# A decoder layer on one Trainium2 core: seven block products in the fourth gate-and-up tile of the FFN too, and the splits it needs in one row

## The chip, the cores and the metric

The kernel runs on 1 core of one Trainium2 chip, as one launch. The metric is the device time of a launch in microseconds (us). Unless said otherwise, times inside a launch are counted from the first instruction of one profiled execution. The engines are called by the profile's names: PE (TensorE matmul) with PEld (its weight load), DVE (VectorE), ACT (ScalarE), POOL (GpSimd) and SP (SyncE, which here issues DMAs).

## What is computed

One layer of a decoder for a prompt of 512 tokens and a sample group of 8 sequences with one token each, 520 tokens in all, width 1024. All tensors are float32. Cut to what matters here:

```python
D_FF = 2816
x = x + g1 * mixed                                    # after the RG-LRU and attention branches, @ w_o
h2 = rms_norm(x, norm2_g) * (1.0 + sc2) + sh2
gu, up = jnp.split(h2 @ w_ffn_in, 2, axis=-1)
x = x + g2 * ((jax.nn.silu(gu) * up) @ w_ffn_out)
y = rms_norm(x, normf_g)
```

## The kernel before, in words

**Layout.** Activations are held transposed, 128 features on the partitions and the 520 tokens along the free dimension, cut into two halves of 260 tokens (`HALVES`). Every matmul is 128x128 weights against 128x260 tokens. Float32 products are made of three fp32r matmuls: weights and activations are each split into a rounded part "hi" (a cast on ACT) and the rest "lo" (a subtraction on DVE), and hi\*hi, lo\*hi and hi\*lo are summed.

**The FFN.** The 2816 gate columns and 2816 up columns are worked in 22 tiles `jt` of 128 gate and 128 up columns. The main loop's head treats tiles 0 and 1 together (names `fi0` to `fi3`, first all four products of the first token half, then all four of the second; meanwhile `rstd_half` and `h2_half(1)`, L1434 to L1458, make the second half of the FFN input `h2`). Tiles 2 and 3 are plain tiles (`ffn_tile`): a gate product `fig` and an up product `fiu`, each of 8 k-tiles x 3 matmuls x 2 halves = 48 matmuls. From tile `GROUP` = 4 on, `fast_tile` (L1588) treats the tile as a 2x2 by 2x2 block product (gate and up columns; the two halves of k; the two halves of the tokens) and needs seven block products of 4 k-tiles x 3 matmuls = 12 matmuls each, in place of eight. The seven stand in the order of `BLOCKS`: A11, S2, S3, S1, A12, A22, S4. Their results meet in four PSUM banks X, Y, W and Z, with two ACT copies and four DVE additions (L1601, L1616, L1622).

**What the seven products need.** On the weight side, four block sums S1 to S4 of each tile, made on POOL by `split_block` (L264 to L267, each 128x512, results in `ws` tiles), and one split of each block into hi and lo by `split_four` (ACT L273, DVE L274, names `wb`). On the activation side, block sums of `h2` in `u` and `w`, made once on POOL by `h2_blocks` (L1580 to L1583, sixteen instructions of 128x260), and their splits `tu` and `tw`, made once by `split_blocks` (ACT L341, DVE L342, eight pairs of 128x520). A11, A12 and S4's activation operands are blocks of `h2` itself; S2 and S3 use `tw`, S1 and A22 use `tu`. S2, the second product of a tile, uses all four `tw`.

**When things are issued.** `begin` asks for the loads and splits of the units that lie ahead: loads 22 and splits 11 in a unit of time near a microsecond. `split_upto(first + m - 1)` at the end of the head already asks for the splits of the next three units. `defer(k, fn)` puts a function behind the k-th product from here. `split_blocks` stands under `issue_after(state["silu"].ins)`: its ACT instructions come behind the last silu before it. Each weight chunk of 1024 rows by 256 columns is loaded by SP into one of two `wraw` buffers; the next chunk but one waits until a buffer's readers are done. Split weights have three `whi` and three `wlo` buffers, `ws` and other large tiles seven (`pg`), most other tiles come from a heap of 60 slots.

**The order on an engine** isn't that of the program text alone: when the program is built, a scheduler that walks through estimated time gives each engine the earliest instruction in the text whose inputs it takes to be ready. On the chip each engine then keeps that order strictly, and waits where an input is late.

From tile 4 on, products `fo` of the second FFN matrix stand behind blocks S2 and A12 (`JOIN`): those in tiles 4 to 7 use the finished tiles 0 to 3, and so on.

Of the kernel before, what the change touches and what calls it, by code (L numbers as in the profile page):

```python
# [65 lines left out]
def kernel(ctx, tc, xT, par, gates, b_f, cst, cse, own, cache_k, cache_v, cache_lf, pt,  # L66
# [13 lines left out]
    def slot(name, cols=NT, dt=F32, parts=128):  # L80
        return heap.tile([parts, cols], dt, name=name, tag="slot")

    def bank(name, parts=128, cols=512):
        return psp.tile([parts, cols], F32, name=name, tag="bank")
# [32 lines left out]
    def cols(src, c0, n=256, k0=0, nk=KT):  # L117
        return [(src, k0, nk, c0, n)]
# [22 lines left out]
    for i in range(0, KT, 2):  # L141
        chunks.append(cols(w_o, 128 * i))
    GROUP = 4
    PLAIN = 2
    LAST = 16
    JOIN = {}
    for jt in range(GROUP, LAST):
        JOIN[jt] = {"S2": (jt // GROUP - 1, 2 * (jt % GROUP)), "A12": (jt // GROUP - 1, 2 * (jt % GROUP) + 1)}
    for i, (jt, name) in enumerate(((16, "S2"), (16, "A12"), (17, "A12"), (18, "A12"), (19, "A12"), (20, "A12"),
                                    (21, "S2"), (21, "A12"))):  # L150
        JOIN.setdefault(jt, {})[name] = (LAST // GROUP - 1, i)
    BLOCKS = ("A11", "S2", "S3", "S1", "A12", "A22", "S4")
    units = []

    def whole(c):
        for o in range(0, sum(p[4] for p in chunks[c]), 128):
            units.append((c, o, chunks[c][0][2]))
# [4 lines left out]
    for jt in range(FF // 128):  # L162
        c = len(chunks)
        chunks.append(cols(w_fi, 128 * jt, 128) + cols(w_fi, FF + 128 * jt, 128))
        if jt < GROUP:
            whole(c)
            continue
        for name in BLOCKS:
            units.append((c, name, 4))
            if name in JOIN[jt]:  # L170
                g, i = JOIN[jt][name]
                if i % 2 == 0:
                    joined.add(len(chunks))
                    chunks.append(cols(w_fo, 128 * i, 256, 128 * GROUP * g, GROUP))
                units.append((max(joined), 128 * (i % 2), GROUP))
    for i in range(0, KT, 2):
# [108 lines left out]
    def defer(k, fn):  # L285
        later.setdefault(state["n"] + k, []).append(fn)

    def begin(last=None):
        n = state["n"]
        state["n"] += 1  # L290
        last = len(units) - 1 if last is None else last
        if n < 42:
            tick(KEYS[n], n in VALUES)
        load_chunks(units[reach(n, last, state["load"])][0])
        split_upto(reach(n, last, state["lead"]))
        flush()
        return n
# [13 lines left out]
    def run_later(n):  # L311
        for fn in later.pop(n, []):
            fn()
# [7 lines left out]
    def product(name, a, evac, mid=None):  # L321
        n = begin()
        for j in range(2):
            b = bank(f"{name}_{j}")
            half_product(n, j, a, b)
            evac(j, b[:, :HALF])
            if j == 0 and mid is not None:
                mid()
        run_later(n)
# [7 lines left out]
    def split(name, raw, scale=None):  # L337
        hi = slot(name + "h", dt=F32R)
        lo = slot(name + "l", dt=F32R)
        if scale is None:  # L340
            act.copy(hi, raw)  # L341
            dve.tensor_tensor(lo, raw, hi.bitcast(F32), ALU.subtract)  # L342
        else:
            act.activation(hi, raw, AF.Copy, scale=scale)
            dve.scalar_tensor_tensor(lo, raw, scale, hi.bitcast(F32), ALU.mult, ALU.subtract)
        return hi, lo
# [1070 lines left out]
    def residual(f, ps, gate, j):  # L1417
        if j == 0:
            dve.scalar_tensor_tensor(x[f][:, :HALF], ps[:, :HALF], mod[:, gate, f, 0:1], x[f][:, :HALF],
                                     ALU.mult, ALU.add)  # L1420
            return
        n = NP - HALF
        t = small("rs", 128, NS)
        dve.tensor_tensor(t, ps[:, n:HALF], mod[:, gate, f, 1:9], ALU.mult)
        dve.scalar_tensor_tensor(x[f][:, HALF:NP], ps[:, :n], mod[:, gate, f, 0:1], x[f][:, HALF:NP],
                                 ALU.mult, ALU.add)
        dve.tensor_tensor(x[f][:, NP:], x[f][:, NP:], t, ALU.add)
# [32 lines left out]
    def split_part(dst, src, part=slice(None)):  # L1460
        hi, lo = dst
        act.copy(hi[:, part], src)
        dve.tensor_tensor(lo[:, part], src, hi[:, part].bitcast(F32), ALU.subtract)
# [34 lines left out]
    def swish(b, t, j):  # L1498
        t0, t1 = HALVES[j]
        state["silu"] = act.activation(t[:, t0:t1], b[:, :HALF], AF.Silu)  # L1500

    def times_up(b, t, j):
        t0, t1 = HALVES[j]
        dve.tensor_tensor(t[:, t0:t1], b[:, :HALF], t[:, t0:t1], ALU.mult)
# [53 lines left out]
    def pair_out():  # L1558
        return slot("ach", dt=F32R), slot("acl", dt=F32R)

    def ffn_tile(jt):
        t, out = slot("sw"), pair_out()
        product(f"fig{jt}", h2, lambda j, b: swish(b, t, j))

        def up(j, b):
            t0, t1 = HALVES[j]
            times_up(b, t, j)
            split_part(out, t[:, t0:t1], slice(t0, t1))

        product(f"fiu{jt}", h2, up)  # L1570
        return out
# [14 lines left out]
    def split_blocks(k0):  # L1586
        with tc.issue_after(state["silu"].ins):
            for k in range(k0, k0 + 2):  # L1588
                u, w = traw[k]
                tb.append((split("tu", u), split("tw", w)))  # L1590

    def h2_block(name, k):
        pair, part = {"A11": (h2[k], L_), "A12": (h2[k + 4], L_), "S4": (h2[k + 4], R_), "S1": (tb[k][0], L_),
                      "S2": (tb[k][1], L_), "S3": (tb[k][1], R_), "A22": (tb[k][0], R_)}[name]
        return [t[:, part] for t in pair]

    def fast_tile(jt, ac):
        sw, cp, u2, out = slot("sw"), slot("cp"), slot("u2", HALF), pair_out()
        X, Y, W, Z = (bank(f"fi{jt}{n}")[:, :HALF] for n in "xywz")
        into = {"A11": X, "S2": Y, "S3": W, "S1": Z, "A12": X, "A22": W, "S4": Z}  # L1600
        add = lambda o_, a_, b_: dve.tensor_tensor(o_, b_, a_, ALU.add)  # L1601

        def close(b, part):
            dve.tensor_tensor(b, b, sw[:, part], ALU.mult)
            split_part(out, b, part)

        for m_, name in enumerate(BLOCKS):
            n = begin()
            hi, lo = splits[n]
            for k in range(4):  # L1610
                ah, al = h2_block(name, k)
                for m, (wt, at) in enumerate(((hi, ah), (lo, ah), (hi, al))):
                    state["mm"] = pe.matmul(into[name], lhsT=wt[k], rhs=at, start=m_ < 4 and k == 0 and m == 0,
                                            stop=k == 3 and m == 2, skip_group_check=m_ > 3)
            if name == "A11":
                act.copy(cp[:, L_], X)  # L1616
            elif name == "S2":
                add(u2, cp[:, L_], Y)
            elif name == "S3":
                add(W, u2, W)  # L1620
            elif name == "S1":
                act.copy(cp[:, R_], Z)  # L1622
                add(Z, u2, Z)
                add(Y, cp[:, R_], W)
            elif name == "A12":
                act.activation(sw[:, L_], X, AF.Silu)
            elif name == "A22":
                close(W, L_)
            elif name == "S4":
                act.activation(sw[:, R_], Z, AF.Silu)  # L1630
                close(Y, R_)
            run_later(n)
            if name in JOIN[jt]:
                g, i = JOIN[jt][name]
                product(f"fo{g}_{i}", ac[GROUP * g:GROUP * g + GROUP], lambda j, b_, i=i: residual(i, b_, 5, j))
        return out

    ac, ts, ready = [], [slot("sw") for _ in range(PLAIN)], []
    u = state["n"]
    for j in range(2):  # L1640
        for m in range(2 * PLAIN):
            if j == 0:
# [10 lines left out]
            if j == 0 and m == 0:  # L1653
                h2_half(1)
            first = u + 2 * PLAIN
            if j == 0:
# [3 lines left out]
    for t in ts:  # L1660
        out = pair_out()
        split_part(out, t)
        ac.append(out)
    for jt in range(PLAIN, FF // 128):
        if jt == PLAIN:
            for k in range(4):
                h2_blocks(k)
            defer(0, lambda: split_blocks(0))
            defer(1, lambda: split_blocks(2))
        ac.append(fast_tile(jt, ac) if jt >= GROUP else ffn_tile(jt))  # L1670
    last_product(ac[LAST:])


# [60 lines left out]
```

## Time and profile before

| | us |
|---|---|
| median of 3 runs | 1031.36 |
| the three runs | 1032.33, 1027.59, 1031.36 |
| the profiled execution's own time | 1029.59 |
| its span, first to last instruction | 1027.9 |

The profile is one execution. Its page gives the busy time of each engine, a picture of the span in 40 slices, and the chain of waits that ended last; further views answer for a stretch of time, an engine or a tile. Rows of a timeline give start, duration, engine, line and operation, the output tile and its inputs, and in brackets how long the engine was idle before and what ended that. PE's rows overlap, since matmuls are pipelined: the time that a group of matmuls takes is read from the chain, which counts from one start to the next.

### The profile page before, as it was taken

What the parts mean: (1) busy time and instruction counts of PE and PEld (TensorE: products, weight loads), DVE (VectorE), ACT (ScalarE), POOL (GpSimd) and SP (SyncE); (2) the same over time, 40 slices, a digit from 0 to 9 for tenths busy, and PEclk for the clock granted to TensorE, in tenths of its full rate; (3) what the DMA queues carried; (4) which work ended last, traced back from release to release, by engine and by line L of the source; (5) the groups of instructions that cost most, each with busy time, mean ns of one, the idle gap of its engine ahead of it and who ended that gap; (6) DMA issues with size and microseconds to landing.
All of it is one profiled execution on the core that took longest, in us unless ns stands there. A gap on an engine that the chain in (4) does not pass through costs nothing.

```text
span 1027.9 us, 21296 instructions
## 1 busy us (share of the span) xinstructions
PE 992.3 (97%) x7994; PEld 918.8 (89%) x7994; DVE 796.8 (78%) x1423; ACT 551.0 (54%) x1132; POOL 328.6 (32%) x424
## 2 busy tenths in 40 slices
PE   4999999999999999999999999999999999999996
PEld 1788989999898988878888989999999999999996
DVE  5446999998989987886756544878888888888864
ACT  4433665857682267776875233565444444445453
POOL 0214511111133235654430001484432433434212
PEclk9899999999999999999999999999999999999998
DMA  9987987878888999988665784324243342333212
GB/s 323 307 280 285 306 290 217 261 233 276 261 254 310 323 314 306 310 259 274 219 235 185 252 302 126 83 62 115 71 124 99 87 124 72 93 104 103 62 63 84
DMA packets 165419, 206.99 MB, mean 201 GB/s; under 512 B 9906, under 2 KB 126146, under 8 KB 165250
## 3 DMA queue, kind: packets, MB, share of 16 engines
q1 hardware_dynamic: 148594, 152.52, 47.9%
q0 software_dynamic: 13040, 46.67, 13.7%
q10 hardware_dynamic: 3680, 6.42, 1.7%
q8 instruction: 63, 1.03, 0.4%
q14 instruction: 42, 0.34, 0.1%
HBM read 192.49 MB, written 13.09 MB: 200 GB/s over the span
## 4 chain that ended last, share of the span: by engine, by line
PE 70%; DVE 14%; DMA 6%; ACT 5%; issue 3%; SPq 0%; POOL 0%; POOLq 0%; DVEq 0%; ACTq 0%
PE fo L308 12%; PE pb L308 4%; PE gb L308 4%; PE ga L308 3%; PE k L308 3%; PE wo L308 3%; PE v L308 3%; DVE wlo L251 2%; DMA wraw<-in_w_in_dram 2%; PE gr L308 2%; PE xr L308 2%; DVE pg L733 2%; PE qp L530 2%; PE pv L818 2%; PE po L1261 2%
## 5 line engine op out<-in xcount | busy, mean ns | idle before, releaser
L249 ACT CAST whi<-wraw 128x1024 fp32r<-128x1024 f32 (+1 forms) x79 | 82.0, 1039 | 121.2 <-PE pb L308 35.1
L251 DVE TENSOR_TENSOR wlo<-wraw,whi 128x1024 fp32r<-128x1024 f32 (+1 forms) x79 | 101.3, 1284 | 32.6 <-ACT whi L249 30.5
L273 ACT CAST wb<-ws 128x512 fp32r<-128x512 f32 x72 | 44.8, 622 | 91.1 <-PE fo L308 63.6
L308 PE MATMUL fo<-ach,wb 128*128 128x260 f32 x512 | 93.3, 282 | 0.0
L685 POOL DMA_DIRECT2D pg<-in_cache_k_dram x74 | 39.4, 533 | 142.7 <-DVE S L734 70.3
L308 PEld LDWEIGHTS fo<-ach,wb 128*128 128x128 f32 x512 | 78.8, 188 | 0.0
L274 DVE TENSOR_TENSOR wb<-wraw,wb 128x512 fp32r<-128x512 f32 x86 | 74.2, 863 | 5.0 <-ACT wb L273 4.4
L274 DVE TENSOR_TENSOR wb<-ws,wb 128x512 fp32r<-128x512 f32 x72 | 65.8, 913 | 14.0 <-ACT wb L273 12.2
L264 POOL TENSOR_TENSOR ws<-wraw 128x512 f32<-128x512 f32 x18 | 26.6, 1480 | 153.8 <-DMA wraw<-in_w_fi_dram 124.8
L308 PE MATMUL fo<-acl,wb 128*128 128x260 f32 x256 | 72.3, 282 | 0.0
L273 ACT CAST wb<-wraw 128x512 fp32r<-128x512 f32 x86 | 53.6, 623 | 32.7 <-ACT cp L1622 5.8
L733 DVE TENSOR_TENSOR pg<-pg,qb 128x1024 f32<-128x1024 f32 x48 | 58.0, 1227 | 2.5 <-DMA pg<-in_cache_k_dram 2.4
L734 DVE TENSOR_REDUCE S<-pg 128x16 f32<-128x1024 f32 x48 | 57.0, 1207 | 0.1
L1218 POOL TENSOR_SCALAR p<-p,mu 128x128 f32<-128x128 f32 (+3 forms) x28 | 36.4, 1310 | 49.2 <-DVE mu L1214 31.3
L308 PEld LDWEIGHTS fo<-acl,wb 128*128 128x128 f32 x256 | 48.2, 188 | 0.0
L1212 ACT ACTIVATE p<-p,mu 128x128 f32<-128x128 f32 (+3 forms) x64 | 35.3, 553 | 15.9 <-DVE mu L1211 15.6
L308 PE MATMUL v<-hh,whi 128*128 128x260 f32 x128 | 37.3, 291 | 1.1 <-DVE pl L1232 1.1
L308 PE MATMUL pb<-oh,whi 128*128 128x260 f32 x128 | 36.7, 287 | 1.0 <-ACT oh L1319 1.0
L308 PE MATMUL k<-hh,whi 128*128 128x260 f32 x128 | 37.3, 291 | 0.0
L308 PE MATMUL gb<-hh,whi 128*128 128x260 f32 x128 | 37.0, 289 | 0.0
L308 PE MATMUL ga<-hh,wlo 128*128 128x260 f32 x128 | 36.3, 284 | 0.7 <-DVE wlo L251 0.7
L308 PE MATMUL pa<-gl,whi 128*128 128x260 f32 x128 | 36.1, 282 | 0.7 <-DVE gl L342 0.7
(1099 smaller groups left out, 3965.8 us busy)
## 6 DMA issues: line engine op xcount, KB each, us to landing
araw<-in_ada_w_dram SPq DMA_DIRECT2D x48, 512.0 KB, 7.0
wraw<-in_w_fi_dram SPq DMA_DIRECT2D x44, 512.0 KB, 4.7
pg<-in_cache_k_dram POOLq DMA_DIRECT2D x42, 512.0 KB, 6.0
pg<-in_cache_v_dram SPq DMA_DIRECT2D x42, 512.0 KB, 5.1
wraw<-in_w_in_dram SPq DMA_DIRECT2D x34, 512.0 KB, 7.8
wraw<-in_w_in_dram SPq DMA_DIRECT2D x11, 1024.0 KB, 10.0
pg<-in_cache_v_dram POOLq DMA_DIRECT2D x22, 512.0 KB, 6.4
pg<-in_cache_k_dram POOLq DMA_DIRECT2D x32, 256.0 KB, 5.7
```

Of the source, the lines that this page charges most:

```text
L249: state["act"] = act.copy(hi[:, :k1 - k0], src)
L251: state["last"] = dve.tensor_tensor(lo[:, :k1 - k0], src, hi[:, :k1 - k0].bitcast(F32), ALU.subtract)
L264: pool.tensor_tensor(s1, a21, a22, ALU.add)
L273: state["act"] = act.copy(t[:, :4], src)
L274: state["last"] = dve.tensor_tensor(t[:, 4:], src, t[:, :4].bitcast(F32), ALU.subtract)
L308: state["mm"] = pe.matmul(out[:, :t1 - t0], lhsT=wt[k], rhs=at, start=k == 0 and m == 0, stop=k == nk - 1 and m == 2)
L530: state["mm"] = pe.matmul(b[:, :HALF], lhsT=wt, rhs=at[:, t0:t1], start=k == 0 and m == 0, stop=k == 3 and m == 2)
L685: done.append(eng.dma_start(pg, cache[bass.ds(r, 1), :, c0:c1].rearrange("a p c -> (a p) c")))
L733: dve.tensor_tensor(pg, pg, q, ALU.mult)
L734: last = dve.tensor_reduce(S[r // 2][:, c:c + H], pg.rearrange("p (h d) -> p h d", d=DH), AX.X, ALU.add)
L1212: act.activation(p[:, :n + 128], p[:, :n + 128], AF.Exp, bias=mu[:, 0:1], scale=-1.0, accum_out=mu[:, 1:2])
L1218: (pool.tensor_scalar(p, p, mu[:, 2:3], None, ALU.mult) if a and i + 1 < KT else act.activation(p, p, AF.Copy, scale=mu[:, 2:3]))
```

## The change

- `FIRST = 3` takes the place of `GROUP` where it is decided which tiles are fast. Tile 3 becomes a fast tile. `GROUP` = 4 stays for the groups of `fo` products.
- The units of tile 3 are seven blocks in place of two plain units, with no `fo` product among them (`JOIN` has no entry for 3).
- Both calls of `split_blocks` stand behind the gate product of tile 2; before, the first call stood there and the second behind its up product.

```diff
     GROUP = 4
+    FIRST = 3
     PLAIN = 2
...
-        if jt < GROUP:
+        if jt < FIRST:
             whole(c)
             continue
...
-            if name in JOIN[jt]:
+            if name in JOIN.get(jt, ()):
...
             run_later(n)
-            if name in JOIN[jt]:
+            if name in JOIN.get(jt, ()):
...
-            defer(0, lambda: split_blocks(0))
-            defer(1, lambda: split_blocks(2))
-        ac.append(fast_tile(jt, ac) if jt >= GROUP else ffn_tile(jt))
+            defer(0, lambda: (split_blocks(0), split_blocks(2)))
+        ac.append(fast_tile(jt, ac) if jt >= FIRST else ffn_tile(jt))
```

## The prediction

> **What bounds the kernel now.** I read the busy table first, then the chain of waits over the stretch where the edit lies (655 to 720 us), then the timelines of POOL, DVE and SP there. The page's busy table:
>
> ```profile
> span 1027.9 us, 21296 instructions
> PE 992.3 (97%) x7994; PEld 918.8 (89%) x7994; DVE 796.8 (78%) x1423; ACT 551.0 (54%) x1132; POOL 328.6 (32%) x424
> ```
>
> PE is the bound over the whole, but the share says nothing about one stage. The chain says which wait ends last (columns: start, duration, what):
>
> ```profile
> 667.30 1.70 DVE r L409
> ...
> 669.52 0.33 POOL h2r L1450
> 669.92 0.28 POOL h2r L1451
> ...
> 677.51 8.44 PE fi L308 x68
> 685.95 5.74 PE fig L308 x48
> 691.68 5.74 PE fiu L308 x48
> 697.42 5.74 PE fig L308 x48
> 703.16 5.74 PE fiu L308 x48
> 708.90 1.43 PE fi4x L1613 x12
> ```
>
> Two things are to be seen. From 677.5 on the chain is PE without a gap: tile 2 (685.95), tile 3 (697.42), tile 4 (708.90, its first block product of seven). So a matmul less there is time less, as long as nothing is late. Before 677.5 the chain is not PE's: it runs through DVE, ACT **and two small POOL instructions**, the making of the second half of `h2`. PE waits for it little by little, and the whole list of PE's waits from 658 us to the end has only two rows beside it (engine, line, what it waited for: us in total, times, longest):
>
> ```profile
> PE r L407 <- DVE ss L400: 1.4, 1, 1.4
> PE fi L308 <- DVE h2l L1458: 1.1, 3, 0.4
> PE r L1536 <- ACT sq L1524: 0.2, 1, 0.2
> ```
>
> **The change part by part.**
>
> *Term 1, the matmuls.* Tile 3 goes from 2 x 48 = 96 matmuls to 7 x 12 = 84. Its chain rows give 5.74/48 = 0.120 us from one matmul to the next, and a block of 12 takes 1.43 to 1.44. So tile 3 takes 10.04 in place of 11.48: **-1.44 us**, 0.14% of the kernel. That is all the change can win; nothing else on the chain becomes shorter.
>
> *Term 2, four more block sums on POOL.* Tile 3 now needs S1 to S4 of its weights. They are asked for at the end of the head (the third of the three units that are split in advance there is now A11 of tile 3, whose call makes all four sums), that is in the text behind `h2_half(1)` and in front of `h2_blocks`. A tile's sums look like this, with what stands on POOL around them:
>
> ```profile
> 669.52 0.32 POOL L1450 TENSOR_TENSOR h2r<-h2r,n2amp 128x8 f32<-128x8 f32 x1 [9.64 <-DVE h2r L1446]
> ...
> 675.50 0.79 POOL L1582 TENSOR_TENSOR w<-h2r 128x260 f32<-128x260 f32 x1
> 676.24 0.92 POOL L1581 TENSOR_TENSOR w<-h2r,u 128x260 f32<-128x260 f32 x1
> ...
> 691.09 1.29 POOL L264 TENSOR_TENSOR ws<-wraw 128x512 f32<-128x512 f32 x1 [0.54 <-DMA wraw<-in_w_fi_dram]
> ...
> 695.43 2.15 POOL L267 TENSOR_TENSOR ws<-wraw,ws 128x512 f32<-128x512 f32 x1
> ```
>
> POOL idles 9.64 us before the first small instruction, and it doesn't keep the text's order: L1582 runs before L1581, which stands ahead of it, because L1581 needs the `u` that L1580 makes. So the scheduler will put the sums into that idle time if it takes tile 3's weights to be there. Are they? SP issues that chunk here, and the table by stretch shows the DMA share (next to last column) fall:
>
> ```profile
> 660.46 0.99 SPq L213 DMA_DIRECT2D wraw<-in_w_fi_dram  x2
> 663.00:665.00 2.00, 1.78 (x13) 1.75 (x14) 0.07 (x1) 1.97 (x3) 0.00 (x0) 1.00 1.18 317
> 665.00:667.00 2.00, 2.00 (x19) 2.00 (x18) 0.13 (x1) 1.09 (x2) 0.00 (x0) 1.00 0.22 50
> ```
>
> 0.22/1.18 of 2 us is 0.4, so the chunk is in at 665.4. Four sums at the undisturbed 1.29 take 5.2 and end at 670.6; at the 6.5 that the four took whose first and last are quoted (691.09 to 697.58) they end at 671.9. The small POOL instruction that is on the chain stands at 669.52. So the second half of `h2` is late by 670.6 - 669.5 = **1.1**, at most 2.4, and by nothing if the scheduler puts the sums behind. From 667.3 to 669.0 DVE works on the reciprocal, with one input, and has little else, so I take the undisturbed price, 1.1. That lateness goes to PE in full, since PE waits for that half already.
>
> *Term 3, the splits must be earlier.* Today `tw` is first used by tile 4's S2 at 708.90 + 1.43 = 710.33; now by tile 3's S2 at 697.42 + 1.44 = 698.86, and its fourth `tw` at the last three of the twelve matmuls, 698.86 + 11 x 0.12 = 700.2 for its lo part. The row of eight splits starts behind the silu of `fig2`:
>
> ```profile
> 691.72 0.39 ACT L1500 ACTIVATE sw<-fig 128x260 f32<-128x260 f32 x1 [2.35 <-PE fig L308]
> 692.66 1.54 DVE L342 TENSOR_TENSOR tul<-u,tuh 128x520 fp32r<-128x520 f32 x1 [2.71 <-ACT tuh L341]
> 694.12 2.32 DVE L251 TENSOR_TENSOR wlo<-wraw,whi 128x1024 fp32r<-128x1024 f32 x1
> 696.36 1.78 DVE L342 TENSOR_TENSOR twl<-w,twh 128x520 fp32r<-128x520 f32 x1
> 698.07 0.41 DVE L1504 TENSOR_TENSOR sw<-fiu,sw 128x260 f32<-128x260 f32 x1
> 698.41 0.68 DVE L342 TENSOR_TENSOR tul<-u,tuh 128x520 fp32r<-128x520 f32 x1
> 699.01 0.69 DVE L342 TENSOR_TENSOR twl<-w,twh 128x520 fp32r<-128x520 f32 x1
> ```
>
> ACT follows at 0.53 a cast and is no limit. A split on DVE takes 0.60 from start to start when POOL rests (698.41 to 699.01), but 1.5 to 1.8 beside POOL's sums of tile 4. Undisturbed, the three long DVE instructions from 692.66 to 698.07 are 0.6 + 1.2 (two 512s) + 0.6 = 2.4 us of work; they took 5.4, a rate of 0.45. Now the eight splits are 4.8 us of work; the weight splits of S3 and S1, which get their buffers when `fig2` ends, add 1.2 if they stand ahead. In the stretch to 698.1 2.4 us of it are done; 2.4 to 3.6 remain and end at 700.5 to 701.7, against 700.2 needed: late by 0.3 to 1.5. I take **1.0**, nearer the upper end, since S3 and S1 stand ahead of the row in the text. Lower end 0, since DVE can also win:
>
> ```profile
> 702.41 4.31 POOL L264 TENSOR_TENSOR ws<-wraw 128x512 f32<-128x512 f32 x1 [4.82 <-DMA wraw<-in_w_fi_dram]
> 702.46 0.68 DVE L274 TENSOR_TENSOR wb<-wraw,wb 128x512 fp32r<-128x512 f32 x1
> 703.06 0.69 DVE L342 TENSOR_TENSOR tul<-u,tuh 128x520 fp32r<-128x520 f32 x1
> ```
>
> Here POOL's sum stretches from 1.29 to 4.31 and DVE keeps its 0.6. At that rate ten splits end at 698.7, in time. Upper end 5.8, in the rival below.
>
> *Edits at nothing.* Tile 3's seven weight splits cost DVE 7 x 0.6 and four additions come on top, but two plain splits (2 x 1.2) and half of the evacuation of a plain tile go. A block of 1.44 us then carries a split of 0.6 and about one more short DVE instruction, as in the fast tiles today, where PE's list of waits has no row. If that cover failed, each of seven blocks would wait a few tenths. A11's weights need no sum and are split before 697. S3 and S1 find buffers at 691.7, A12 and A22 when `fiu2` frees one at 697.4, 5.8 us before A12 is due. SP's loads:
>
> ```profile
> 685.26 0.99 SPq L213 DMA_DIRECT2D wraw<-in_w_fi_dram  x2
> ...
> 696.47 0.99 SPq L213 DMA_DIRECT2D wraw<-in_w_fi_dram  x2
> ```
>
> The issue at 696.47 (tile 5) waits for tile 3's raw weights; their last reader is now A22's split, some 700 to 702. The chunk lands about 6 later (POOL's L264 at 702.41 waited for this issue), its sums take 6.5, and tile 4 lasts 7 x 1.44 and two `fo` products, so tile 5's S2 is due some 17 after tile 4's first block at 707.5: slack of about 10. Behind it on SP stands only the next `fo` chunk, due later still. Tile 4's `ws` now take buffers that `h2_blocks` has read, which POOL has finished by then in its own order. `fo` of tile 4 reads tile 3's result two blocks (2.9 us) after its last, as tile 8 does with tile 7's today, also without a wait.
>
> *Sum.* -1.44 + 1.1 + 1.0 = **+0.7**. The profiled execution takes 1029.59 by its own time (span 1027.9 and 1.7 around it), so it would become 1030.3; the median of the runs shown lies 1.8 above the profiled one, and from there the forecast is **1032.0**.
>
> **The rivals.**
>
> 1. *Both covers hold.* The sums stand behind the small POOL instructions or fit in the 4 us of idle time, and DVE wins against POOL. For it: the 0.60 pitch at 702. Against: the 0.45 rate at 692. Then -1.44 remains: 1029.9.
>
> 2. *POOL falls behind and DVE pays (slower).* The sums of tile 3 run behind `h2_blocks`, at 690.5, and tile 4's follow until about 703. The row of ten splits then runs at the rate 0.45 throughout: 6.0/0.45 = 13.3, from 692.7 to 706.0, and S2 waits 5.8; term 2 falls away. -1.44 + 5.8 = +4.4: 1035.7. It decides only if the sums aren't put into the idle time and POOL, not DVE, keeps its pace. The Trainium skill, "GPSIMD Engine Reference", section 1, says that GpSimd shares its SBUF interfaces with VectorE and contends with instructions of two SBUF inputs. By that rule every split of the row would be met by every sum, which is this rival; the trace agrees, at 692 on DVE (1.54 against 0.68) and at 702 on POOL (4.31 against 1.29).
>
> 3. *The sums stand in the middle of the small POOL instructions (slower).* The scheduler puts them behind the first `h2r` because the next isn't ready, and the chain through POOL gets all four: 6.5, with term 3: -1.44 + 6.5 + 1.0 = +6.1, or 1037.4. For it: the swapped order of L1582 and L1581 shows that such gaps are used. Against: the weights are there 4 us before the first `h2r`, so most sums find room ahead. It decides once at least three of the four stand behind 669.5.
>
> 4. *The change doesn't do what it says*: tile 3 takes 11.5 still, because each block waits about 0.2 for DVE; no other term. 1031.4.
>
> **How the numbers follow.** Chances: forecast (net between -0.5 and +3) 0.50; rival 1 0.22; rival 2 0.13; rival 3 0.10; rival 4 0.05. A measurement of this kernel tells about 0.5% from no change, 5.2 us; the three runs alone lie 4.7 apart. Faster by more would need what no case gives, so 0.02 for the scatter. Slower by more is above 1036.5: rival 3, and a little of rival 2, 0.12. The rest, 0.86, is within. The range reaches from rival 1 by the profiled execution's own time (1028.2) to rival 2 with a little scatter, 1036.5; rival 3 is left out.
>
> **What would show it.** Term 1: twelve-matmul rows `fi3x`, `fi3y`, ... of 1.44 in the chain where tile 3 had 5.74 twice. Term 2: four L264 to L267 sums near 665 to 671, the small `h2r` on POOL starting later than 669.5 against the end of its DVE input, and PE's waits for `h2l` above 1.1. Term 3: a wait of PE in `fi3y` for `twl`, and the eighth split ending behind 700. Wrong I would be if the sums appear elsewhere than at 665 or behind `h2_blocks`, or if PE waits at a place not named here: for a weight split in tile 4, or a bank.

## The result, and the profile after

The changed kernel takes 1038.48 us (median, 1034.66 to 1044.4); the kernel before, run beside it, 1033.26 (1027.59 to 1036.63). The ratio is **1.0057 (95% interval 1.004 to 1.0074)**: slower, by 5.2 us between the medians, where +0.7 was forecast, and the time lies above the range of 1028.2 to 1036.5. Of the 6.5 us between the forecast 1032.0 and 1038.48, 1.9 belong to the kernel before, which here ran at 1033.26 and not at the 1031.36 on which the forecast stands. The profiled execution takes 1037.17 by its own time. Its busy table (line numbers of the changed kernel are one higher than before):

```profile
span 1034.2 us, 21298 instructions
PE 994.8 (96%) x7982; PEld 919.7 (89%) x7982; DVE 801.4 (77%) x1432; ACT 553.9 (54%) x1139; POOL 332.1 (32%) x428
```

PE has 12 instructions less and yet 2.5 us more busy time; POOL has the four sums more. To place the loss, take three marks in PE's timeline: the first matmul of the head (`fi`), of tile 2 (`fig`), and of tile 5's second product (`fi5y`). First in the kernel before, then in the changed one:

```profile
658.79 0.28 PE L308 MATMUL fi<-h2h,whi 128*128 128x260 f32 x1
...
685.78 0.28 PE L308 MATMUL fig<-h2h,whi 128*128 128x260 f32 x1
...
725.97 0.40 PE L1613 MATMUL fi5y<-twh,wb 128*128 128x260 f32 x2
```

```profile
659.46 0.28 PE L309 MATMUL fi<-h2h,whi 128*128 128x260 f32 x1
...
688.48 0.28 PE L309 MATMUL fig<-h2h,whi 128*128 128x260 f32 x1
...
732.18 0.40 PE L1614 MATMUL fi5y<-twh,wb 128*128 128x260 f32 x2
```

The head takes 29.02 in place of 26.99 (**+2.03**), tiles 2 to 4 with the first block of 5 take 43.70 in place of 40.19 (**+3.51**); 0.67 was there before the head began, where nothing is changed, and behind `fi5y` the two spans end alike. So the experiments below are read by these two lengths, which don't carry the scatter of the rest of the kernel; each is taken from one profiled execution.

The first two rows of PE's waits from 600 us on (total, times, longest); the two others are those of before:

```profile
PE fi3y L1614 <- DVE twl L343: 2.4, 3, 1.5
PE fi L309 <- DVE h2l L1459: 2.3, 5, 0.6
```

Both new waits stand where the prediction put them: `h2l` 2.3 in place of 1.1, and a new one, S2 of tile 3 for `twl`.

**The head.** POOL's timeline, the first and the last of the four sums and the first small instruction, which stood at 669.52:

```profile
666.97 1.29 POOL L265 TENSOR_TENSOR ws<-wraw 128x512 f32<-128x512 f32 x1 [6.40 <-DMA wraw<-in_w_fi_dram]
...
670.85 1.36 POOL L268 TENSOR_TENSOR ws<-wraw,ws 128x512 f32<-128x512 f32 x1
672.16 0.39 POOL L1451 TENSOR_TENSOR h2r<-h2r,n2amp 128x8 f32<-128x8 f32 x1
```

The four sums run in the idle time, at the undisturbed pace. From the head's first matmul the small instruction starts at 672.16 - 659.46 = 12.70, before at 10.73: 1.97 later, and that is the head's loss.

**Tile 3.** PE's S2 and DVE's row:

```profile
702.47 0.39 PE L1614 MATMUL fi3y<-twl,wb 128*128 128x260 f32 x1 [0.32 <-DVE twl L343]
...
705.85 0.39 PE L1614 MATMUL fi3y<-twl,wb 128*128 128x260 f32 x1 [1.53 <-DVE twl L343]
```

```profile
694.95 3.58 DVE L275 TENSOR_TENSOR wb<-ws,wb 128x512 fp32r<-128x512 f32 x2 [1.63 <-ACT wb L274]
698.45 1.79 DVE L343 TENSOR_TENSOR tul<-u,tuh 128x520 fp32r<-128x520 f32 x1
700.17 0.69 DVE L343 TENSOR_TENSOR twl<-w,twh 128x520 fp32r<-128x520 f32 x1
700.78 0.41 DVE L1505 TENSOR_TENSOR sw<-fiu,sw 128x260 f32<-128x260 f32 x1
...
703.56 0.41 DVE L1505 TENSOR_TENSOR sw<-fiu,sw 128x260 f32<-128x260 f32 x1
...
704.50 0.68 DVE L275 TENSOR_TENSOR wb<-wraw,wb 128x512 fp32r<-128x512 f32 x1
705.10 0.69 DVE L343 TENSOR_TENSOR twl<-w,twh 128x520 fp32r<-128x520 f32 x1
```

Two weight splits stand ahead of the row and take 3.58 instead of 1.2, the first split of the row 1.79 instead of 0.69; from 700.17 on, DVE has its pace of 0.6. But the row isn't made of splits alone: two products `sw` of tile 2's evacuation (0.34 each, from start to start) and a third weight split (0.60) stand in it. The stretched part falls in the time in which POOL makes tile 4's sums:

```profile
693.70 1.31 POOL L265 TENSOR_TENSOR ws<-wraw 128x512 f32<-128x512 f32 x1 [0.93 <-DMA wraw<-in_w_fi_dram]
...
698.06 1.63 POOL L268 TENSOR_TENSOR ws<-wraw,ws 128x512 f32<-128x512 f32 x1
```

So (3.58 - 1.2) + (1.79 - 0.69) = 3.5 us of DVE's time went to the meeting with POOL. The products of tile 3 in the chain:

```profile
706.23 2.13 PE fi3w L1614 x12
708.36 2.27 PE fi3z L1614 x12
710.63 1.43 PE fi3x L1614 x12
```

S2 begins at 701.39 and S3 at 706.07: 4.68 for a block of 1.44, **3.24 lost**. And the two blocks behind it take 2.13 and 2.27, though PE waits for nothing: **1.52 more**. The table by stretch tells why (width, busy time of PE, PEld, DVE, ACT, POOL with their counts, then the granted TensorE clock, the DMA share and GB/s):

```profile
704.00:706.00 2.00, 0.47 (x4) 0.26 (x3) 2.00 (x4) 0.41 (x1) 0.00 (x0) 1.00 0.00 0
706.00:707.00 1.00, 1.00 (x8) 1.00 (x9) 1.00 (x3) 0.69 (x2) 0.00 (x0) 0.84 0.00 0
707.00:708.00 1.00, 1.00 (x7) 1.00 (x6) 1.00 (x3) 0.21 (x1) 0.00 (x0) 0.50 0.20 53
...
710.00:711.00 1.00, 1.00 (x10) 1.00 (x10) 0.17 (x1) 0.33 (x1) 0.00 (x0) 0.95 1.16 292
```

Behind the wait the granted clock falls to 0.50 for some 3.3 us. The sum of the stage is -1.44 + 3.24 + 1.52 = 3.32 of the 3.51 measured.

### The profile page after: what moved, and what is told of

Read it like the earlier page. It is cut to its first block, busy times and chain, and to the rows that moved or that the text cites. A ratio compares the mean times of both kernels' runs of the same rounds, so it can differ in the third digit from the quotient of the medians.

```text
span 1034.2 us, 21298 instructions
## 1 busy us (share of the span) xinstructions
PE 994.8 (96%) x7982; PEld 919.7 (89%) x7982; DVE 801.4 (77%) x1432; ACT 553.9 (54%) x1139; POOL 332.1 (32%) x428
## 4 chain that ended last, share of the span: by engine, by line
PE 74%; DVE 12%; DMA 5%; ACT 4%; issue 2%; POOL 1%; SPq 0%; DVEq 0%; POOLq 0%; ACTq 0%
PE fo L309 12%; PE pb L309 4%; PE gb L309 4%; PE k L309 4%; PE v L309 3%; PE ga L309 3%; DMA wraw<-in_w_in_dram 3%; PE pa L309 3%; PE wo L309 3%; PE gr L309 2%; PE xr L309 2%; PE pv L819 2%; PE qp L531 2%; DVE wlo L252 2%; PE po L1262 2%
## 5 line engine op out<-in xcount | busy, mean ns | idle before, releaser
L250 ACT CAST whi<-wraw 128x1024 fp32r<-128x1024 f32 (+1 forms) x77 | 79.9, 1040 | 120.2 <-PE pb L309 35.1
L252 DVE TENSOR_TENSOR wlo<-wraw,whi 128x1024 fp32r<-128x1024 f32 (+1 forms) x77 | 95.3, 1239 | 31.1 <-ACT whi L250 29.0
L274 ACT CAST wb<-ws 128x512 fp32r<-128x512 f32 x76 | 47.2, 622 | 94.8 <-PE fo L309 63.3
L275 DVE TENSOR_TENSOR wb<-ws,wb 128x512 fp32r<-128x512 f32 x76 | 69.8, 920 | 16.6 <-ACT wb L274 14.7
L275 DVE TENSOR_TENSOR wb<-wraw,wb 128x512 fp32r<-128x512 f32 x89 | 77.6, 872 | 6.4 <-ACT wb L274 5.9
```

Source lines behind the costliest of these rows:

```text
L250: state["act"] = act.copy(hi[:, :k1 - k0], src)
L252: state["last"] = dve.tensor_tensor(lo[:, :k1 - k0], src, hi[:, :k1 - k0].bitcast(F32), ALU.subtract)
L274: state["act"] = act.copy(t[:, :4], src)
L275: state["last"] = dve.tensor_tensor(t[:, 4:], src, t[:, :4].bitcast(F32), ALU.subtract)
```

## The experiments

**Theory.** The loss is POOL's sums beside DVE (head: in front of the small instructions; tile 3: beside the row), and half clock behind PE's wait. **Rivals**: the one row is what costs, whatever tile 3 is; DVE has too much to do for a fast tile 3 in any order; the splits only stand in the wrong order. "Head" and "tiles 2-4" are the two lengths from above; the ratio is to the kernel before on the same chip, where there is no interval, one time stands with before's median beside it.

| kernel | head | tiles 2-4 | ratio (95% interval), or one time |
|---|---|---|---|
| before | 26.99 | 40.19 | |
| after | 29.02 | 43.70 | 1.0057 (1.004 to 1.0074) |
| row_only | 26.98 | 40.20 | 1.0006 (0.9987 to 1.0025) |
| w_first | 29.17 | 43.26 | 1.005 (1.0027 to 1.0073) |
| sums_behind | 29.94 | 46.63 | 1.0083 (1.0052 to 1.0114) |
| no_sums4 | 29.02 | 39.27 | 1031.82 (before 1030.84) |
| sums4_late | 29.08 | 45.72 | 1.0062 (1.0039 to 1.0085) |
| two_and_two | 27.01 | 45.96 | 1.0058 (1.0038 to 1.0077) |
| two_calls | 31.21 | 43.72 | 1044.25 (before 1031.85) |
| late_row | 27.01 | 41.26 | 1030.19 (before 1031.85) |
| head_only | 27.06 | 46.53 | 1.0048 (1.0029 to 1.0066) |
| dve_sums4 | 26.99 | 43.48 | 1.0037 (1.0019 to 1.0055) |
| a12_dve_sums4 | 27.01 | 43.42 | 1.0036 (1.0021 to 1.0051) |
| free_a12_dve | 26.99 | 42.18 | 1.0014 (0.9999 to 1.0028) |

**row_only**: the one row without the fast tile 3.

```diff
-    FIRST = 3
+    FIRST = 4
```

> Tile 3 is a plain tile again; only the eight splits of u and w stand in one row behind tile 2's gate product. Theory (three prices: POOL's sums ahead of the small h2 instructions +2.0, S2's wait for tw +3.2, PE at half clock behind that wait +1.5, against -1.44 for twelve matmuls): none of the three is left, PE waits for h2l about 1.1 in all and for nothing after 678, the time is that of before within 0.2%. Rival 'the row itself': eight splits in a row hold up times_up and the weight splits behind them, PE waits in tile 3 or 4, 2 us or more slower than before.

Both lengths are those of before to 0.01. The row by itself costs nothing; that rival falls.

**w_first**: the four `tw` ahead of the four `tu`.

```diff
-            for k in range(k0, k0 + 2):
-                u, w = traw[k]
-                tb.append((split("tu", u), split("tw", w)))
+            tw = [split("tw", traw[k][1]) for k in range(k0, k0 + 4)]
+            tu = [split("tu", traw[k][0]) for k in range(k0, k0 + 4)]
+            tb.extend(zip(tu, tw))
...
-            defer(0, lambda: (split_blocks(0), split_blocks(2)))
+            defer(0, lambda: split_blocks(0))
```

> As the changed kernel, but in the row the four splits of w come first and those of u behind. Theory: the first four splits of the row ended at 702.4 in the changed kernel, S2 wants its last one at 702.7; so S2 waits 0.5 at most, the half clock goes with the wait, and from the start of tile 2's gate product to S2 of tile 4 it is 4 to 4.7 us less (about 23.5 in place of 27.9). The head's waits for h2l stay at 2.3. About level with before or up to 0.1% above. Rival 'the fast tile itself': DVE has too much to do here in any order, S1 then waits for tu or a weight split for DVE, and less than 2 us come back.

PE no longer waits in S2, but at tile 3's last product S4, for the additions that DVE makes between the products:

```profile
PE fi3z L1614 <- DVE fi3z L1602: 2.3, 1, 2.3
```

Half clock follows there too (0.69 at 712 to 714, 0.50 at 714 to 716). Only 0.44 of the 3.51 came back. The order was not the cause: what is saved in S2 is late some 8 us on, since DVE has no idle time from 698 to 712.

**sums_behind**: tile 3's (and every tile's) sums not before the last small POOL instruction of `h2_half(1)`.

```diff
+            with tc.issue_after(state["tail"].ins):
                 pool.tensor_tensor(s1, a21, a22, ALU.add)
...
-                pool.tensor_tensor(t[:, NP:], t[:, NP:], b_[:, 1:9], ALU.add)
+                state["tail"] = pool.tensor_tensor(t[:, NP:], t[:, NP:], b_[:, 1:9], ALU.add)
```

> As the changed kernel, but POOL's four block sums of tile 3 are ordered behind the small h2 instructions of the second half (and ahead of u and w). Theory: the small instructions start about 669.6 again after the end of their input, the waits for h2l fall from 2.3 to about 1.1, and the head is 2.0 us shorter; u and w end some 5 us later against the head, S2's wait stays near 3.2 or grows by up to 1: 1 to 2 us less than the changed kernel. Rival 'contention': the sums now run beside the last h2l subtractions on DVE and stretch them, and the head is no shorter.

The head became 0.92 longer instead of shorter: the sums now run at 676.6 to 681.9 beside the last `h2l`, which DVE makes from two inputs:

```profile
675.79 0.77 DVE L1460 TENSOR_TENSOR h2l<-h2r,h2h 128x260 fp32r<-128x260 f32 x2
...
677.93 2.90 DVE L1460 TENSOR_TENSOR h2l<-h2r,h2h 128x260 fp32r<-128x260 f32 x2
```

PE's wait for `h2l` rises to 2.7. All of POOL shifts, tile 4's sums run until 704.1, PE's waits in S2 add up to 3.2 (2.4 in after), and S4 waits another 0.8. Moved sums meet other DVE work: DVE pays, as in the prediction's rival 2.

**no_sums4**: tile 4's four sums are left out and its products take raw blocks, so part of tile 4 isn't computed.

```diff
+            if state["tiles"] == 2:
+                blocks.update(S1=a21, S2=a11, S3=a12, S4=a22)
+                return split_four(blocks[name])
```

> As the changed kernel, but tile 4's four block sums are left out (its products take raw blocks in their place, so part of the computation is missing), and POOL is idle while DVE works on the row of splits. Theory (DVE is slowed by POOL's sums, not by its own load): the two weight splits ahead of the row take 1.2 in place of 3.6, the row runs at 0.6 a split, the fourth tw is done by about 702, S2 waits under 0.8 and the half clock goes: about 4 us from tile 2 to tile 4. Rival 'DVE's own load': the row ends no earlier than 704 and S2 waits 2 or more.

The row without POOL beside it:

```profile
695.34 1.29 DVE L279 TENSOR_TENSOR wb<-ws,wb 128x512 fp32r<-128x512 f32 x2 [1.66 <-ACT wb L278]
696.66 0.70 DVE L347 TENSOR_TENSOR tul<-u,tuh 128x520 fp32r<-128x520 f32 x1
...
702.22 0.69 DVE L347 TENSOR_TENSOR twl<-w,twh 128x520 fp32r<-128x520 f32 x1
```

The two splits take 1.29 for 3.58. Counted from the first matmul of `fig` (688.87 here) the last `twl` starts at 13.35; in after at 705.10 - 688.48 = 16.62. Tile 3 has no wait, the clock stays at 1.00, and tiles 2-4 take 0.92 less than before. So without these four sums tile 3 loses nothing, though all other work of the row still stands on DVE (its two `sw` and the third weight split too), and most of term 1 is there. The head keeps its 2 us: the two losses have separate causes.

**sums4_late**: nothing left out; tile 4's sums come behind a small POOL copy that reads the last split of the row.

```diff
+            if state["tiles"] == 2:
+                mark = small("mark", 128, NS, 1)
+                state["mark"] = pool.tensor_copy(mark, tb[3][1][1][:, :NS].bitcast(F32))
+                gate = tc.issue_after(state["mark"].ins)
+            with gate:
```

> As the changed kernel, nothing left out, but POOL starts tile 4's four block sums only when DVE has done the last split of the row (a small POOL copy reads that split first, and the sums stand behind it). Theory (POOL's sums slow the row): as where tile 4's sums were left out, the row runs at 0.6 a split, S2 of tile 3 waits under 0.3 and the half clock goes; the sums then run some 703 to 709.5 and their splits are due at about 710.5, so tile 4 may wait up to 1. Against the changed kernel 4 to 5 us less; the head's 2.0 stays: level with before within 0.2%. Rival 'only postponed': the sums beside tile 3's additions and weight splits slow DVE there just as much, PE waits 2 or more in tile 3 or 4, and less than 2 us come back.

S2 no longer waits. The sums run at 705.9 to 712.0 and stretch what stands on DVE then, and the next splits wait for them:

```profile
706.52 2.98 DVE L1471 TENSOR_TENSOR acl<-sw,ach 128x260 fp32r<-128x260 f32 x2
...
711.33 1.21 DVE L282 TENSOR_TENSOR wb<-ws,wb 128x512 fp32r<-128x512 f32 x1 [1.48 <-ACT wb L281]
712.46 0.42 DVE L1609 TENSOR_TENSOR fi3w<-fi3w,u 128x260 f32<-128x260 f32 x1
```

The `acl` pair takes 2.98 (0.76 in w_first), the addition at 712.46 stands in DVE's order behind a split of a sum that POOL has only just made, and PE waits 4.7 at S4 (`fi3z`), again with half clock behind it. The loss was only put off.

**two_and_two**: as sums4_late, and of tile 3's sums only S1 and S3 ahead of the small instructions, S2 and S4 behind `u` and `w`.

```diff
+                if state["tiles"] == 1:
+                    state["rest"] = rest
...
+            with tc.issue_after(state["block"].ins):
+                state["rest"]()
```

> As the one before, and of tile 3's four sums only S1 and S3 stand ahead of the small h2 instructions (room 667.0 to 669.5), S2 and S4 behind u and w. Theory: the small instructions start about 0.3 behind their input in place of 2.5, the head loses its 2.0, and with no wait left in tile 3 the 1.44 of the twelve matmuls come out: 0.1 to 0.2% faster than before, 6 to 7 us faster than the changed kernel. Rival 'contention goes along': the head stays 1 us or more long, since DVE's four products of x and r beside the two sums are stretched as they were beside four (3.5 in place of 1.5).

The head is 27.01, with `h2l` at 1.1: two sums of 1.25 less in front of the small instructions bring its 2 us back. But the wait at `fi3z` stays, 4.6, and the time doesn't fall below after's.

**two_calls**: the two calls of `split_blocks` as before, with the fast tile 3.

```diff
-            defer(0, lambda: (split_blocks(0), split_blocks(2)))
+            defer(0, lambda: split_blocks(0))
+            defer(1, lambda: split_blocks(2))
```

> As the changed kernel, but the splits stand in two calls as before, the second behind tile 2's up product. Theory: the third and fourth tw come behind fiu2 and its evacuation, some 1 to 3 us later than in the one row, so S2 of tile 3 waits 4 to 6 and the half clock lasts as long: 1 to 3 us slower than the changed kernel. Rival 'the row is what costs': with the old order the waits shrink and it is faster than the changed kernel by 2 or more.

Tiles 2-4 take 43.72, as in after: so the one row is no help against two calls here, nor a harm, and neither the theory nor its rival holds. Its waits differ (1.4 in S2, 0.7 at `fi3w`). The head's 31.21 and a late start of the head make this single execution 1044.25; why its head is longer than after's is not settled.

**late_row**: tile 3 plain, the row behind tile 3's up product.

```diff
-    FIRST = 3
+    FIRST = 4
...
-            defer(0, lambda: (split_blocks(0), split_blocks(2)))
+            defer(3, lambda: (split_blocks(0), split_blocks(2)))
```

> Tile 3 is plain as before; all eight splits stand behind tile 3's up product, so that tile 4's S2 has to wait for them, in a kernel with no seven-product tile 3. Theory of the clock: PE waits some 2 to 5 us there, the granted clock falls to about 0.5 for 3 to 4 us right behind the wait, and those matmuls take twice as long (1.5 to 2 us on top). Rival 'the half clock belongs to the changed order of PE's work in tile 3': the clock stays at 1.00 behind the wait.

It was meant to make a wait of PE by lateness alone and to see the clock fall. The scheduler put `fo` products between the matmuls of tile 4's S2, PE waited 0.2, the clock stayed at 1.00. Tiles 2-4 take 1.07 more than before, of which the list of waits names only that 0.2. The question was not answered by it.

**head_only**: two_and_two without the delay of tile 4's sums.

```diff
+            def rest():
+                eng.tensor_tensor(s2, s1, a11, ALU.subtract)
+                eng.tensor_tensor(s4, a12, s2, ALU.subtract)
...
+            if state["tiles"] == 1:
+                state["rest"] = rest
```

> As the changed kernel, with only the head mended: of tile 3's four sums S1 and S3 stand ahead of the small h2 instructions, S2 and S4 behind u and w; tile 4's sums run on POOL as soon as they can. Theory: the head is 2.0 us shorter (h2l waits 1.1), while the row of splits still meets POOL's sums (now S2 and S4 of tile 3 and then four of tile 4): S2 of tile 3 waits 3 to 4 in all, the half clock follows, 1 to 2 us less than the changed kernel and still 0.3 to 0.5% above before. Rival 'one backlog': the head was the cause of the later wait, and with it mended the row is in time.

The head gives its 2.0 back, tiles 2-4 lose 2.8 more than in after. PE's waits in S2 add up to 4.0, and behind them the chain has:

```profile
708.10 2.60 PE fi3w L1623 x12
710.70 2.60 PE fi3z L1623 x12
713.30 1.58 PE fi3x L1623 x12
```

PE comes to tile 3 2 us earlier, DVE's row doesn't; half clock now costs 6.78 - 4.32 = 2.46 (three blocks of 1.44 are 4.32). Both lengths together are 73.59, after's 72.72. An early wait that is taken away is found again at the next thing that is late.

**dve_sums4**: as head_only, tile 4's sums on DVE.

```diff
-            eng = pool
+            eng = dve if state["tiles"] == 2 else pool
```

> As the one before, and tile 4's four block sums are made on DVE in place of POOL (nothing left out). Theory (what DVE loses beside four POOL sums, about 3 us, is more than the sums' own 4 x 0.6 on DVE): DVE makes them in the gap ahead of the row, when tile 4's weights land, the row then runs at 0.6 a split, the last tw is ready about 704, S2 waits 0.5 to 1.2 with no half clock behind it; from the start of tile 2's gate product to tile 4's S2 about 24 us as before, the head as before: level with before, -0.1 to +0.1%. Rival 'DVE is full': 2.4 us more work delays the row as much as POOL did, S2 waits 3 or more.

POOL rests from 694 to 710 and the row has the pitch 0.61. But the four sums take DVE 3.8 us (691.66 to 695.50), as much as the meeting with POOL did, and counted from `fig` (686.47) the last `twl` starts at 702.85 - 686.47 = 16.38, after's 16.62. PE waits 2.1 in S2, with half clock behind it (0.56 and 0.58 from 704 to 708). The 2 us of the head are won, and next to nothing in tile 3.

**a12_dve_sums4**: as dve_sums4, with A12 in the program's text as tile 3's second product, so that S2 would be due 1.44 later.

```diff
+    EARLY = ("A11", "A12", "S2", "S3", "S1", "A22", "S4")
...
-        for name in BLOCKS:
+        for name in EARLY if jt == FIRST else BLOCKS:
```

> As the one before, and tile 3 takes its products in the order A11, A12, S2, S3, S1, A22, S4, so that two products that need no split of the row (2.9 us in place of 1.4) stand ahead of S2. Theory: S2 waits at most 0.2, nothing else waits, and the 1.44 of the twelve matmuls come out: 0.1 to 0.15% faster than before. Rival 'the wait moves on': DVE's additions of tile 3 come behind the weight splits, and PE waits 1 or more at S4 or in tile 4.

PE didn't take that order. The rows in which the products begin:

```profile
699.05 0.39 PE L1627 MATMUL fi3x<-h2h,wb 128*128 128x260 f32 x2
...
700.48 0.40 PE L1627 MATMUL fi3y<-twh,wb 128*128 128x260 f32 x2
...
705.96 0.51 PE L1627 MATMUL fi3x<-h2h,wb 128*128 128x260 f32 x2
```

A12 adds to the bank that A11 has filled, behind ACT's copy of it, and the scheduler put S2 and most of S3 in between. So the wait in S2 is that of dve_sums4 to 0.01 (0.60 and 1.54 for 0.59 and 1.53), and the run says nothing on a later S2. It says something else: the clock stays at 1.00 here, and 1.1 of what that saves goes into waits before `fo` (0.7 and 0.4, for `ach` and `acl`).

**free_a12_dve**: as a12_dve_sums4, the row no longer held behind the silu.

```diff
     def split_blocks(k0):
-        with tc.issue_after(state["silu"].ins):
-            for k in range(k0, k0 + 2):
+        for k in range(k0, k0 + 2):
```

> As the last one (S2 and S4 of tile 3 behind u and w, tile 4's sums on DVE, A12 ahead of S2), and the row of splits isn't held behind the silu of tile 2's gate product any more, so that ACT and DVE take its first splits where they idle. Theory (what is short is time on DVE between u and w and S2, and nothing else): two of the eight splits move ahead of the weight splits, the last tw is ready about 702.5 by the clock of the run before, S2 waits under 0.3, no half clock, fo of tile 4 waits under 0.5: from tile 2's gate product to tile 5's S2 39 to 39.5 us in place of 40.2, 0.05 to 0.12% faster than before. Rival 'DVE is full here in any order': the waits come back at fi3y, fi3z or fo with 2 us or more in all, and it is not faster than before.

The best of those with a fast tile 3 and nothing left out: 1.0014, not to be told from before. DVE (third busy column) has hardly a gap:

```profile
690.00:694.00 4.00, 4.00 (x35) 4.00 (x35) 3.84 (x4) 3.46 (x8) 2.42 (x2) 1.00 0.32 108
694.00:698.00 4.00, 4.00 (x36) 4.00 (x35) 4.00 (x8) 1.21 (x3) 0.00 (x0) 1.00 0.00 0
698.00:702.00 4.00, 2.66 (x21) 2.25 (x20) 4.00 (x8) 2.24 (x5) 0.00 (x0) 1.00 0.00 0
702.00:704.00 2.00, 2.00 (x19) 2.00 (x18) 1.94 (x5) 1.41 (x4) 0.00 (x0) 1.00 0.15 42
```

It is busy 13.78 of 14 us, and PE still waits three times for 0.7 to 0.8, in S2, at A12 (for ACT's copy; A12 stands in the middle of S2 here) and before `fo`. Tiles 2-4 take 2.0 more than before. So the second rival holds beside the theory, for every order tried: **the work of DVE and POOL together is too much for this place**. With the sums on POOL they stretch DVE; with them on DVE, DVE is full. Only no_sums4, which does less, let the shorter tile through. No version tried that has a fast tile 3 and computes all of it beats the kernel before.

## Why the prediction was wrong

*Term 1* was right: with nothing late (no_sums4) tile 3's first four blocks take 1.43 or 1.44 each, and 12 matmuls less are 12 less.

*Term 2* had its place and mechanism right, and 2.0 lies in its bounds of 0 to 2.4. The sums took 5.24 as worked out; the chunk landed 7.51 behind the head's first matmul, not the 6.61 that I read from the DMA share. The fall of the share wasn't the landing: in the kernel before it is 0.02 from 665.5 to 666.0, but the second half of the chunk, issued by SP at 660.9, lands 5.3 later, at 666.2, and that is 7.4 behind the head's first matmul. This is the 0.9 between 1.1 and 2.0.

*Term 3* is **the step that failed: "I take 1.0", where S2 of tile 3 lost 3.24 and the clock behind it another 1.52.** The wait was the one named, at the place named, and even the order (S3 and S1 ahead of the row) was foreseen. So was what POOL's sums take from DVE: by the forecast 2.4 us of the ten splits' work are done at 698.1, 12.3 behind the first matmul of `fig`, and in the changed kernel two weight splits and two of the row are done at 700.78, also 12.3 behind it. What failed is the rest of the row. The six splits left were counted as 3.6 us, late by 1.5, and of that I took 1.0. But DVE's order puts three more instructions among them, two `sw` and a weight split of a raw block, 1.3 us in all. The forecast knew this work and charged it nowhere, though the trace of before has such instructions between its splits:

```profile
699.96 0.41 DVE L1504 TENSOR_TENSOR sw<-fiu,sw 128x260 f32<-128x260 f32 x1
...
700.91 0.68 DVE L274 TENSOR_TENSOR wb<-ws,wb 128x512 fp32r<-128x512 f32 x1
```

So the 2.2 that are missing are 0.5 by my choice inside the range, 1.3 by these three, and 0.4 because PE came to S2 0.2 earlier than forecast and 0.2 passed between the end of the split and the matmuls behind it. Without POOL's 3.5 none of this would show: in no_sums4 the same three instructions stand in the row, and without the sums it is in time. The lower end of the term rested on DVE's winning side (702 in before), which didn't occur in the changed kernel's row.

*The clock* has no term in the prediction. The trace of before shows it, in a stretch that I had not read, at the start of the kernel:

```profile
24.00:26.00 2.00, 0.18 (x3) 0.02 (x1) 1.70 (x6) 1.93 (x5) 1.22 (x3) 0.83 1.09 356
26.00:28.00 2.00, 2.00 (x9) 1.97 (x10) 1.90 (x5) 2.00 (x5) 1.76 (x6) 0.50 1.05 386
...
30.00:32.00 2.00, 2.00 (x14) 1.36 (x7) 2.00 (x3) 0.33 (x2) 0.00 (x0) 0.50 1.07 392
32.00:34.00 2.00, 2.00 (x20) 1.45 (x20) 0.89 (x2) 0.00 (x0) 0.00 (x0) 0.96 1.02 379
```

PE works 0.18 of 2 us and then has 0.50 of its clock for 6 us. A wait of a few us can have such a tail, and a forecast with a possible wait of 5.8 should have had one.

*"Edits at nothing"* was wrong as a whole in one point: DVE's work in tile 3 was held to be hidden since fast tiles today show no wait. Today's fast tiles begin after the row (in before its last split ends at 704.4, tile 4 begins at 708.9); tile 3 begins in the middle of it. w_first shows the additions late as soon as S2 isn't.

*The rivals.* The sum of +4.4 for rival 2 came near the measured +5.2, but by another way: the sums of tile 3 didn't run behind `h2_blocks` and the head lost 2.0. Its mechanism, DVE paying for POOL's sums, is what happened, for the first three of the ten splits. Rival 3 didn't occur: all four sums ran before the first small instruction. Rivals 1 and 4 fell with the waits.

From forecast to profile: +0.7 forecast, +0.9 in term 2, +2.2 in term 3's wait, +1.5 of clock, 0.2 unplaced: +5.5 by the two lengths, 5.2 by the medians.

## What to carry to other kernels

Before a deadline, count everything that stands in the engine's order, and not only the work that the change moves there. Where two engines slow one another, add up the work of both in that stretch as if one engine did it. Give each forecast wait of PE of a few us a possible tail of clock, and read the tail's price from any gap that the trace already has. A wait taken away early is only won if what is late next comes earlier too: look who sets the next deadline before adding two gains.

## What the runs showed of the hardware

**One at a time.** Beside POOL's sums a DVE instruction of two inputs comes every 1.7 to 1.8 us instead of 0.6 (3.58 for two; 698.45 to 700.17), and POOL's sum every 1.84 instead of 1.25 (696.22 to 698.06): about 0.6 + 1.25, as if they took turns. The Trainium skill, "SBUF — State Buffer", section "Who interferes with whom", states that a DVE instruction with two SBUF inputs contends with a GpSimd instruction that reads SBUF, and that the contention is an exclusive lock. The trace agrees; in before, at 702.41, POOL was the one that was held (4.31).

**Half clock behind a wait, but not behind every one.** It followed PE's waits in after, w_first, sums_behind, sums4_late, two_and_two, two_calls, head_only and dve_sums4. It did not in a12_dve_sums4, with the same two waits in S2 as in dve_sums4. First the stretch of dve_sums4, then that of a12_dve_sums4:

```profile
702.00:704.00 2.00, 0.47 (x4) 0.41 (x4) 2.00 (x4) 0.16 (x1) 0.00 (x0) 1.00 0.00 0
704.00:706.00 2.00, 2.00 (x12) 2.00 (x12) 2.00 (x5) 0.90 (x2) 0.00 (x0) 0.56 0.20 58
```

```profile
702.00:704.00 2.00, 0.62 (x3) 0.42 (x3) 2.00 (x5) 0.41 (x1) 0.00 (x0) 1.00 0.00 0
704.00:706.00 2.00, 1.47 (x12) 1.42 (x12) 2.00 (x5) 0.89 (x2) 0.00 (x0) 1.00 0.00 0
```

No single wait in after was longer than 1.53, so one long gap isn't needed. In sums4_late and two_and_two PE waits 4.7 and 4.6 at the same place; the clock falls within the wait in the first (0.57 at 712 to 714) and only at its end in the second (1.00 there, 0.70 at 714 to 716). The Trainium skill, "TensorE: Matmul & The Clock Gate", Part 1, has two states, half clock after an idle window of about 3.4 us, full after as long a busy one, the window running freely. The tail agrees (0.50 for some 3.3 us in after); a wholly idle window of 3.4 us was not needed. A free-running window would let the same wait once be met and once not; that fits both pairs above, but no run here shows the window, and from which idle share the clock falls stays open.
